# The last norm in two token tiles, and the experts' first query made one token tile at a time

## The chip, the cores and the metric

The kernel runs on one core of one Trainium2 chip. The metric is the device time of one execution in microseconds (us), the median of several. A profiled execution has a time of its own, and a span, which is the time from its first to its last recorded instruction. The engines are TensorE (PE: matmuls; PEld: its weight loads, which run beside the matmuls), VectorE (DVE), ScalarE (ACT), GpSimd (POOL) and SyncE (SP), which here issues every DMA.

## The reference, cut to what matters

256 tokens of 1024 features in float32 pass two attention layers, a third layer with windowed and neighbourhood attention, and then a layer of experts. The change lies between the third layer's output projection and the experts' first query:

```python
x = x + gate1[:, None, :] * (mixed @ w_out[layer])
h2 = modulate(rms_norm_2(x, norm2_g[layer]), shift2, scale2)
x = x + gate2[:, None, :] * peer(h2, w_query[layer], sub_keys[layer], u_experts[layer], v_experts[layer])
# in peer, per token: qh = xc @ w_query        (8 heads of 256)
#                     s1, s2 = qh halves against sub_keys, top 16 of each, top 16 of their sums
#                     z = xc @ u_sel ; a = gelu(z) * g ; out = a @ v_sel
```

The kernel does not gather experts: it computes z for all 128 x 128 experts (128 "u tiles") and multiplies by gains that are zero where an expert was not chosen.

## The kernel before, in words

The 256 tokens are two token tiles t = 0 and 1 of 128. The residual `x[t]` lies with tokens on partitions; the normed input `h` lies transposed, features on partitions, in 8 chunks k of 128 features, all 256 tokens along the free axis. A product in float32 accuracy is made of three matmuls (`mm3`, L239 to L241) of rounded halves: hi by hi, hi by lo, lo by hi. A weight from memory is loaded into one of 4 `raw` buffers (L229) and split: ScalarE casts hi (L186), VectorE subtracts lo = raw - hi (L211). There are 4 pairs of `hi`/`lo` buffers; further ones (`mo`) come from `more`.

The order of the work around the change:

- **The output projection** is `out_half(1)`. For t = 0, 1 and for c = 0, 1 (512 columns each) it makes 12 matmuls and then `finish(t, c, y)`: y times the row factor times the gate (L1280), x += y (L1283), and on ScalarE the square of x with its row sum (L262). Below, "the gate product" and "the add" of a (t, c) are L1280 and L1283.
- **The last norm** is `norm_T(5)`. For each t, `norm_diag` makes the reciprocal root of the sums in eight tiny VectorE operations (`rstd_x`, L271 to L278) and a diagonal matrix of it (L518). `norm_x` multiplies x with that matrix on TensorE, which scales and transposes (L525: 8 products for a token tile, two matmul records each, in two PSUM tiles of four feature chunks, called k4 = 0 and 1). `norm_h` applies scale and shift (k4 = 0 on ScalarE, L538; k4 = 1 on VectorE, L540) and splits the result into `hh` (L187 or L186) and `hl` (L211).
- **The experts' stage** `peer` first stores x in memory (L1351), loads constants and the keys (L1362, L1382), and makes `query(0)`: `projT` takes `wq[0]`, four split tiles of two feature chunks each, as the stationary operand and h as the moving one, 8 chunks x 2 halves m x 3 = 48 matmuls of 256 columns (all tokens). After it come u tile 0 (24 matmuls of 256 columns), the scores of query 0 (L1398), u tile 1, and so on without a break to the end of the kernel.

Tile's planner sets each engine's order of issue: among the operations that are ready in its model the one with the lowest priority number goes first, and the number grows in the order of the program. The layer's steps are listed in `ORDER['2']`; its last step, `O@5`, is `out_half(1)` with its numbers raised by 250, so that what comes after it in the program (the norm, the splits of `wq[0]`) goes ahead of it wherever it is ready. `add_manual_dep(..., NoSync, ...)` only puts one instruction behind another in the order of issue of the same engine; it adds no semaphore.

Of the kernel before, what the change touches and what calls it, by code (L numbers as in the profile page):

```python
# [15 lines left out]
OP = mybir.AluOpType  # L16
# [5 lines left out]
NK = 8  # L22
# [127 lines left out]
class Net:  # L150
    def __init__(self, ctx, tc, a):
        self.ctx, self.tc, self.nc, self.a = ctx, tc, tc.nc, a
        self.evn = 0
        self.spare = []
        self.oacc = {}
        self.paced = None
        self.lasts = []
        self.mods = {}
        self.ssx = None
# [36 lines left out]
    def split(self, raw, n=512, more=None):  # L196

        if more is None:
            hi = self.st.tile([128, 512], F32R, name="hi", tag="hi", bufs=self.nhl)
            lo = self.st.tile([128, 512], F32R, name="lo", tag="lo", bufs=self.nhl)  # L200
        else:
            hi, lo = more()
        i = self.split_to(hi[:, :n], lo[:, :n], raw[:, :n])
        self.lasts.append(i)
        if self.paced:
            self.paced(i)
        return hi, lo
# [306 lines left out]
    def norm_diag(self, t):  # L514

        self.rstd_x(self.rs[:, t:t + 1], self.ssx[:, 0, t:t + 1], self.ssx[:, 1, t:t + 1])
        dg = self.wp.tile([128, 128], F32, name="diag", tag="cpt", bufs=self.B("cpt"))
        self.nc.vector.tensor_scalar(dg, self.c("ident"), self.rs[:, t:t + 1], None, op0=OP.mult)  # L518
        return dg

    def norm_x(self, t, k4, dg):
# [20 lines left out]

    def norm_T(self, mod, ahead):

        self.norm_prep()
        for t in range(2):
            dg = self.norm_diag(t)
            pss = [self.norm_x(t, k4, dg) for k4 in range(2)]
            if t == 0:
                next(ahead)  # L550
            for k4 in range(2):
                self.norm_h(t, k4, pss[k4], mod, "av"[k4])
        self.ssx = None
        return self.h
# [42 lines left out]
    def proj(self, h, w, n=512):  # L597

        acc = [self.acc()[:, :n] for _ in range(2)]
        if isinstance(w, bass.AP):  # L600
            order = ((t, k, wt) for k, wt in enumerate(self.tiles(w, n)) for t in range(2))
        else:
            ws = next(w)
            order = ((t, k, wt) for t in range(2) for k, wt in enumerate(ws))
        for t, k, wt in order:
            self.mm3(acc[t], h, wt, (slice(None), k, slice(t * 128, t * 128 + 128)),
                     (slice(None), slice(0, n)), k == 0, k == NK - 1)
        return acc

    def projT(self, h, w, ps):  # L610

# [531 lines left out]
    def block2(self):  # L1143
        nc, v, a = self.nc, self.nc.vector, self.a
        with ExitStack() as es:
# [5 lines left out]
            h = self.norm_T(3, first)  # L1151
# [95 lines left out]
            def v_b():  # L1247
                o1 = self.proj(h, W[3])
                for t in range(2):
# [2 lines left out]
            self.steps("2", {"pA": ka_va, "qa": qa, "kb": kb, "qb": qb, "tb": tb, "vb": v_b, "sa": s_a, "sb": s_b,  # L1252
                             "oa": o_a, "ob": o_b})
            h = self.norm_T(5, iter([None]))
        for t in range(2):
            self.dump(f"x3_{t}", self.x[t])
        return self.gr, h

    def out_half(self, i):

        v = self.nc.vector
        oz, w, ssp = self.oz, self.wo, self.ssp
        if i == 0:
            self.gate = self.gate_rows(self.gr, self.ghalf)
        gate = self.gate
        rs = None
        if ssp is not None:
            rs = self.sm.tile([128, 2], F32, name="rab", tag="rab", bufs=2)
# [8 lines left out]
        def finish(t, c, y):  # L1277
            sl = slice(512 * c, 512 * c + 512)
            if rs is not None:
                v.scalar_tensor_tensor(y, y, rs[:, t:t + 1], gate[:, sl], op0=OP.mult, op1=OP.mult)  # L1280
            else:
                v.tensor_tensor(y, y, gate[:, sl], op=OP.mult)
            v.tensor_tensor(self.x[t][:, sl], y, self.x[t][:, sl], op=OP.add)  # L1283
            if i == 1:
                self.square(y, self.x[t][:, sl], self.ssx[:, c, t:t + 1])

# [2 lines left out]
        if i == 0:  # L1289
            for c in range(2):  # L1290
                acc = [self.acc() for _ in range(2)]
                for kw in weights(c):
                    for t in range(2):
                        product(t, [kw], acc[t])
                for t in range(2):
                    if merged:
                        self.oacc[t, c] = acc[t]
                    else:
                        finish(t, c, acc[t])
        else:  # L1300
            self.ssx = self.sm.tile([128, 2, 2], F32, name="ssx", tag="ssx", bufs=2)
            ws = [list(weights(0)), list(weights(1, self.more))]
            for t in range(2):
                for c in range(2):
                    acc = self.oacc[t, c] if merged else self.acc()
                    product(t, ws[c], acc)
                    finish(t, c, acc)

    def b2_out(self, t, ab, o, oz, ssp):
        nc, v = self.nc, self.nc.vector  # L1310
# [32 lines left out]
    def peer(self, r4, h):  # L1343
        nc, v, a = self.nc, self.nc.vector, self.a
# [16 lines left out]
        o, w = _CST["iota"]  # L1361
# [16 lines left out]
        with ExitStack() as er:  # L1378
# [9 lines left out]
            def query(hd):  # L1388

                acc = self.ps()  # L1390
                self.projT(h, a["wq"][hd], acc)
                qh = wp.tile([128, 2, 256], F32, name="qh", tag="qh", bufs=2)
                nc.scalar.copy(qh.rearrange("p a b -> p (a b)"), acc)
                uu(1)
# [288 lines left out]
```

## Time and profile before

| | |
|---|---|
| median of 3 runs | 1391.97 us (1389.85 to 1392.41) |
| the profiled execution: its time / its span | 1390.83 us / 1389.1 us |
| PE busy | 1339.5 us, 96% of the span, 8842 matmuls |
| PEld busy | 1126.9 us, 81% |
| DVE / ACT / POOL busy | 1023.2 us (74%) / 820.2 us (59%) / 21.8 us (2%) |
| granted TensorE clock, mean | 0.99 |
| DMA | 279.17 MB, mean 201 GB/s |

All times below are microseconds from the start of the span. A row of the timeline gives start, length, engine, line, operation, output tile <- input tiles, shapes and how many instructions were merged into the row; in square brackets stands how long the engine was idle before it, and what released it. A matmul's recorded length is its latency: matmuls are pipelined, and the distance from one start to the next says what one costs in a stream. PEclk is the TensorE clock that the throttle granted: 1.00 is 2.4 GHz, 0.50 is 1.2 GHz, and a value between says how much of the stretch lay at either level.

### The profile page before, as it was taken

What the parts mean: (1) busy time and instruction counts of PE and PEld (TensorE: products, weight loads), DVE (VectorE), ACT (ScalarE), POOL (GpSimd) and SP (SyncE); (2) the same over time, 40 slices, a digit from 0 to 9 for tenths busy, and PEclk for the clock granted to TensorE, in tenths of its full rate; (3) what the DMA queues carried; (4) which work ended last, traced back from release to release, by engine and by line L of the source; (5) the groups of instructions that cost most, each with busy time, mean ns of one, the idle gap of its engine ahead of it and who ended that gap; (6) DMA issues with size and microseconds to landing.
All of it is one profiled execution on the core that took longest, in us unless ns stands there. A gap on an engine that the chain in (4) does not pass through costs nothing.

```text
span 1389.1 us, 25082 instructions
## 1 busy us (share of the span) xinstructions
PE 1339.5 (96%) x8842; PEld 1126.9 (81%) x8842; DVE 1023.2 (74%) x2636; ACT 820.2 (59%) x1887; POOL 21.8 (2%) x27
## 2 busy tenths in 40 slices
PE   6998999999989997999999999999999999999997
PEld 2576775587667756999999999999998888888885
DVE  3595865688576657899999868888866666677777
ACT  3354666367457664555555668888865555555554
POOL 0000000000001100000000000000000000000001
PEclk9999999999999998999999999999999999999999
DMA  8688654742586774555555575455466656667773
GB/s 302 213 283 306 218 188 149 246 157 94 207 296 204 227 236 154 173 179 179 173 180 182 168 217 177 158 166 171 158 224 209 190 192 196 197 222 242 245 242 118
DMA packets 94876, 279.17 MB, mean 201 GB/s; under 512 B 11112, under 2 KB 30320, under 8 KB 94624
## 3 DMA queue, kind: packets, MB, share of 16 engines
q1 hardware_dynamic: 94752, 277.59, 60.6%
q8 instruction: 69, 1.13, 0.3%
q14 instruction: 55, 0.45, 0.1%
HBM read 267.80 MB, written 13.94 MB: 203 GB/s over the span
## 4 chain that ended last, share of the span: by engine, by line
PE 77%; DVE 3%; DMA 2%; ACT 1%; issue 0%; ACTq 0%; DVEq 0%
PE ps L241 18%; PE ps L240 18%; PE ps L239 18%; PE ps L1501 4%; PE acc L241 3%; PE acc L240 3%; PE acc L239 3%; DMA raw<-in_w1o 1%; PE psa L396 1%; PE ps L714 1%; PE ps L525 1%; DVE lo L211 1%; PE ps L709 1%; PE ps L1125 1%; PE ps L639 1%; PE ps L1398 1%
## 5 line engine op out<-in xcount | busy, mean ns | idle before, releaser
L186 ACT CAST hi<-raw 128x512 fp32r<-128x512 f32 (+1 forms) x700 | 429.4, 618 | 350.8 <-PE ps L240 147.8
L211 DVE TENSOR_TENSOR lo<-raw,hi 128x512 fp32r<-128x512 f32 (+1 forms) x700 | 479.8, 688 | 171.2 <-ACT hi L186 158.4
L239 PE MATMUL ps<-hh,hi 128*128 128x256 f32 x1160 | 333.6, 288 | 1.2 <-DVE hh L187 1.2
L240 PE MATMUL ps<-hl,hi 128*128 128x256 f32 x1160 | 329.0, 284 | 1.1 <-DVE hl L211 1.1
L241 PE MATMUL ps<-hh,lo 128*128 128x256 f32 x1160 | 329.0, 284 | 0.0
L239 PEld LDWEIGHTS ps<-hh,hi 128*128 128x128 f32 x1160 | 223.2, 192 | 1.4 <-DVE hh L187 1.4
L240 PEld LDWEIGHTS ps<-hl,hi 128*128 128x128 f32 x1160 | 223.1, 192 | 1.3 <-DVE hl L211 1.3
L241 PEld LDWEIGHTS ps<-hh,lo 128*128 128x128 f32 x1160 | 222.9, 192 | 0.0
L239 PE MATMUL ps<-hi,Ah 128*128 128x512 f32 x508 | 198.1, 390 | 0.0
L240 PE MATMUL ps<-lo,Ah 128*128 128x512 f32 x508 | 197.7, 389 | 0.0
L241 PE MATMUL ps<-hi,Al 128*128 128x512 f32 x508 | 197.6, 389 | 0.0
L240 PEld LDWEIGHTS ps<-lo,Ah 128*128 128x128 f32 x508 | 95.4, 188 | 20.2 <-DVE lo L211 0.2
L239 PEld LDWEIGHTS ps<-hi,Ah 128*128 128x128 f32 x508 | 95.4, 188 | 19.9 <-issue 0.2
L241 PEld LDWEIGHTS ps<-hi,Al 128*128 128x128 f32 x508 | 95.3, 188 | 19.8
L1500 ACT ACTIVATE og<-o,gT 128x128 f32<-128x128 bf16 x256 | 87.2, 394 | 4.1 <-DVE o L1498 0.3
L239 PE MATMUL acc<-hi,hh 128*128 128x512 f32 (+1 forms) x176 | 69.8, 402 | 4.3 <-DVE hh L187 3.1
L240 PE MATMUL acc<-lo,hh 128*128 128x512 f32 (+1 forms) x176 | 70.6, 402 | 2.4 <-DVE lo L211 2.4
L241 PE MATMUL acc<-hi,hl 128*128 128x512 f32 (+1 forms) x176 | 70.2, 400 | 0.0
L1501 PE MATMUL ps<-og,o 128*128 128x128 f32 x512 | 65.1, 275 | 0.0
L1501 PEld LDWEIGHTS ps<-og,o 128*128 128x128 f32 x512 | 61.4, 192 | 0.0
L396 PE MATMUL psa<-adaw,cond 128*32 128x256 f32 x640 | 48.5, 390 | 4.7 <-DMA adaw<-in_adaw 4.3
L1498 DVE TENSOR_TENSOR o<-iof,eT 128x512 bf16<-128x512 f32 x64 | 44.2, 691 | 8.2 <-ACT og L1500 7.5
(397 smaller groups left out, 1937.3 us busy)
## 6 DMA issues: line engine op xcount, KB each, us to landing
raw<-in_u SPq DMA_DIRECT2D x128, 512.0 KB, 3.5
raw<-in_v SPq DMA_DIRECT2D x128, 512.0 KB, 3.5
adaw<-in_adaw SPq DMA_DIRECT2D x86, 512.0 KB, 4.8
raw<-in_w SPq DMA_DIRECT2D x48, 512.0 KB, 3.6
raw<-in_wq SPq DMA_DIRECT2D x16, 512.0 KB, 3.5
zd<-ge SPq DMA_DIRECT2D x56, 128.0 KB, 1.7
ge<-zd SPq DMA_DIRECT2D x56, 128.0 KB, 3.4
raw<-in_adaw SPq DMA_DIRECT2D x10, 512.0 KB, 3.2
```

Of the source, the lines that this page charges most:

```text
L186: return self.nc.scalar.copy(out, in_)
L211: return self.nc.vector.tensor_tensor(lo, src, hi.bitcast(F32), op=OP.subtract)
L239: mm(out, a[0][asl], b[0][bsl], start=first, stop=False, **kw)
L240: mm(out, a[0][asl], b[1][bsl], start=False, stop=False, **kw)
L241: mm(out, a[1][asl], b[0][bsl], start=False, stop=last, **kw)
L396: i = nc.tensor.matmul(ps[32 * q:32 * q + 32, h * 256:h * 256 + 256], self.cond[:, ci + k, :], raw[:, q * 256:q * 256 + 256], start=(k == ...
L525: self.nc.tensor.matmul(ps[:, k * 128:k * 128 + 128], self.x[t][:, k4 * 512 + k * 128:k4 * 512 + k * 128 + 128], dg, start=(k == 0), stop= ...
L639: nc.tensor.transpose(pr[:P, i * 128:i * 128 + 128], s.rearrange("p a d -> p (a d)") if P == 128 else s, self.identr)
L709: nc.tensor.transpose(ps[:, r * 128:r * 128 + 128], P[a][r][:, br, kb, :], self.c("ident"))
L1498: v.tensor_tensor(o1, iob, eT[0][:, t0:t0 + 4, None].to_broadcast([128, 4, 128]), op=OP.is_equal)
L1500: nc.scalar.activation(og[:, j], o1[:, j], AF.Copy, scale=gT[:, t0 + j:t0 + j + 1])
L1501: nc.tensor.matmul(ps[:, j * 128:j * 128 + 128], o2[:, j], og[:, j], start=(j == 0), stop=(j == 3), skip_group_check=True)
```

## The change

`out_half(1)` of the third layer now makes, after the finishes of token tile 0, the norm's preparation and `norm_diag(0)`, so that this tile's diagonal (`dg0`) comes inside the output projection. The gate products of token tile 1 are put behind this diagonal in VectorE's order of issue. The first four splits after the norm (those of `wq[0]`) have their lo put behind the last add of token tile 0. `norm_T` uses the diagonal that is there and makes only the one of token tile 1. `query(0)` goes through `projT_first`: it splits all four tiles of `wq[0]` first, and then makes the product for the 128 tokens of t = 0 over all chunks, and after it for t = 1: 8 x 2 x 3 = 48 matmuls of 128 columns for each token tile, 96 in all.

```diff
@@ split
         i = self.split_to(hi[:, :n], lo[:, :n], raw[:, :n])
         self.lasts.append(i)
+        if self.behind:
+            self.tc.add_manual_dep(i.ins, self.behind.pop().ins.name, mybir.DependencyInfo(
+                mybir.DependencyClass.NoSync, mybir.DependencyReason.DATA), reason="order of issue")
@@ norm_diag
-        self.nc.vector.tensor_scalar(dg, self.c("ident"), self.rs[:, t:t + 1], None, op0=OP.mult)
+        self.diag0 = self.nc.vector.tensor_scalar(dg, self.c("ident"), self.rs[:, t:t + 1], None, op0=OP.mult)
@@ norm_T
-        self.norm_prep()
+        if self.dg0 is None:
+            self.norm_prep()
         for t in range(2):
-            dg = self.norm_diag(t)
+            dg = self.dg0 if t == 0 and self.dg0 is not None else self.norm_diag(t)
@@ new
+    def projT_first(self, h, w, ps):
+        ws = [wt for k4 in range(2) for _, wt in self.load_w(w[k4])]
+        for t in range(2):
+            for k in range(NK):
+                for m in range(2):
+                    o = 256 * m + 128 * t
+                    self.mm3(ps[:, o:o + 128], ws[k // 2], h, (slice(None), slice(k % 2 * 256 + m * 128, k % 2 * 256 + m * 128 + 128)),
+                             (slice(None), k, slice(t * 128, t * 128 + 128)), t == 0 and k == 0 and m == 0,
+                             t == 1 and k == NK - 1 and m == 1, skip_group_check=True)
@@ block2
             h = self.norm_T(5, iter([None]))
+            self.behind = [self.x0] * 4
@@ out_half, finish
-                v.scalar_tensor_tensor(y, y, rs[:, t:t + 1], gate[:, sl], op0=OP.mult, op1=OP.mult)
+                m = v.scalar_tensor_tensor(y, y, rs[:, t:t + 1], gate[:, sl], op0=OP.mult, op1=OP.mult)
+                if t and i == 1:
+                    self.tc.add_manual_dep(m.ins, self.diag0.ins.name, mybir.DependencyInfo(
+                        mybir.DependencyClass.NoSync, mybir.DependencyReason.DATA), reason="order of issue")
...
-            v.tensor_tensor(self.x[t][:, sl], y, self.x[t][:, sl], op=OP.add)
+            add = v.tensor_tensor(self.x[t][:, sl], y, self.x[t][:, sl], op=OP.add)
+            if t == 0:
+                self.x0 = add
@@ out_half, the loop over t
                     product(t, ws[c], acc)
                     finish(t, c, acc)
+                if t == 0 and self.L == 2:
+                    self.norm_prep()
+                    self.dg0 = self.norm_diag(0)
@@ peer, query
-                self.projT(h, a["wq"][hd], acc)
+                (self.projT if hd else self.projT_first)(h, a["wq"][hd], acc)
```

## Rows read from the trace of the kernel before

**Rows 1.** The page: span, and each engine's busy time.
```profile
span 1389.1 us, 25082 instructions
PE 1339.5 (96%) x8842; PEld 1126.9 (81%) x8842; DVE 1023.2 (74%) x2636; ACT 820.2 (59%) x1887; POOL 21.8 (2%) x27
```

**Rows 2.** Stretches: start:end length, busy time (instructions) per engine, clock, DMA share, GB/s.
```profile
560.00:1380.00 820.00, 820.00 (x5500) 758.67 (x5499) 650.39 (x1413) 511.51 (x1135) 3.00 (x3) 1.00 0.59 191
...
535.35:540.27 4.92, 0.00 (x0) 0.03 (x1) 4.77 (x18) 2.05 (x6) 0.00 (x0) 0.82 0.82 311
540.27:546.50 6.23, 6.22 (x32) 6.04 (x32) 3.29 (x11) 2.29 (x7) 0.00 (x0) 0.59 0.62 205
546.50:549.25 2.75, 0.39 (x2) 0.19 (x1) 2.41 (x6) 1.23 (x4) 0.00 (x0) 0.91 0.01 3
549.25:552.00 2.75, 2.75 (x13) 2.75 (x14) 1.28 (x3) 0.78 (x2) 0.00 (x0) 0.50 0.00 0
552.00:559.02 7.02, 7.02 (x59) 7.02 (x59) 3.35 (x5) 3.42 (x6) 0.00 (x0) 0.99 0.29 81
```

**Rows 3.** TensorE's timeline, 535 to 560.
```profile
540.27 6.23 PE L525 MATMUL ps<-diag,x 128*128 128x128 f32 x32 [4.94 <-DVE rx L274]
...
552.19 0.28 PE L241 MATMUL ps<-hh,lo 128*128 128x256 f32 x1
...
559.15 1.06 PE L1398 MATMUL ps<-keys,qh 128*128 128x128 f32 x8
```

**Rows 4.** Waits of PE from 535 to 565: waiter, releaser, total, times, longest.
```profile
PE ps L525 <- DVE rx L274: 4.9, 1, 4.9
PE ps L239 <- DVE hh L187: 1.2, 1, 1.2
PE ps L240 <- DVE hl L211: 1.1, 1, 1.1
```

**Rows 5.** VectorE's timeline, 530 to 552.
```profile
530.50 0.76 DVE L1280 SCALAR_TENSOR_TENSOR acc<-acc,rab,gate 128x512 f32<-128x512 f32 x1
531.17 2.80 DVE L211 TENSOR_TENSOR lo<-raw,hi 128x512 fp32r<-128x512 f32 x4
...
535.80 1.28 DVE L1283 TENSOR_TENSOR x<-acc,x 128x512 f32<-128x512 f32 x2
...
539.28 0.21 DVE L271 TENSOR_SCALAR rx<-ssx 128x1 f32<-128x1 f32 x1
...
539.84 0.29 DVE L518 TENSOR_SCALAR diag<-ident,rstd 128x128 f32<-128x128 f32 x1
...
541.13 0.29 DVE L518 TENSOR_SCALAR diag<-ident,rstd 128x128 f32<-128x128 f32 x1
...
544.56 0.68 DVE L211 TENSOR_TENSOR hl<-hf,hh 128x512 fp32r<-128x512 f32 x1
...
550.52 0.69 DVE L211 TENSOR_TENSOR hl<-hf,hh 128x512 fp32r<-128x512 f32 x1 [0.68 <-ACT hh L186]
```

**Rows 6.** ScalarE's timeline, 530 to 563.
```profile
530.50 2.73 ACT L186 CAST hi<-raw 128x512 fp32r<-128x512 f32 x4 [3.08 <-PE acc L241]
534.60 0.60 ACT L262 ACTIVATE acc<-x 128x512 f32<-128x512 f32 x1 [1.36 <-DVE x L1283]
...
551.83 0.62 ACT L186 CAST hi<-raw 128x512 fp32r<-128x512 f32 x1 [1.34 <-PE ps L240]
```

**Rows 7.** TensorE's timeline in the second layer: matmuls of 128 columns.
```profile
340.67 0.50 PE L733 MATMUL ps<-kT,qT 128*128 128x128 f32 x3
...
307.75 0.22 PE L733 MATMUL ps<-kT,qT 128*128 128x128 f32 x1
307.80 0.45 PE L240 MATMUL acc<-lo,hh 128*128 128x512 f32 x1
```

**Rows 8.** SyncE's DMA issues, 530 to 570.
```profile
536.51 2.32 SPq L1351 DMA_DIRECT2D xd<-x  x2
...
539.34 0.88 SPq L1382 DMA_DIRECT2D keys<-in_keys  x1
```

More of the change, by code (lines that the diff above doesn't have):

```diff
@@ L156, in __init__ @@
         self.paced = None
+        self.behind = []
+        self.dg0 = None
         self.lasts = []
```

## The prediction

> **What bounds the kernel now.** I read the page first: TensorE is busy for 96% of the span [rows 1], so nothing counts that does not shorten TensorE's own work or one of its few gaps. Next come the stretches: from 560 to 1380 TensorE is busy for 820.00 of 820.00 us at full clock [rows 2]. Whatever happens before 560 is therefore worth exactly the shift of the moment at which this unbroken stream begins. I put that moment, E, at the first matmul of u tile 0, which follows the 48 of query 0. From 552.19 on, the fifteenth of them [rows 3], matmuls start every 7.02 / 59 = 0.119 us [rows 2]; the forty-ninth is 34 later, so E = 552.19 + 34 x 0.119 = 556.2. The scores at 559.15, behind the 24 of u tile 0, confirm it: 559.15 - 24 x 0.119 = 556.3 [rows 3]. I use 556.2.
>
> The stretches and TensorE's waits then say what lies ahead of E. TensorE has nothing to do from 535.35 to 540.27, waits 4.9 us for the reciprocal root of the norm, makes the norm of both token tiles in 6.23 us, and waits once more for hh (1.2) and hl (1.1) [rows 2, 4]. VectorE is busy for 4.77 of the 4.92 us of the long wait [rows 2]: this gap is VectorE's work, not a latency. It has two parts there that the change can move: the four lo of the first query's weights, 2.80 us from 531.17, which push the first add back, and the finishes of token tile 1, which lie ahead of the chain of tile 0 [rows 5]. The clock is part of the price: it falls within the long wait (0.82), is 0.59 over the norm, and again 0.50 when the query goes on at 549.25 [rows 2].
>
> **The change part by part.**
>
> *The first diagonal earlier.* Before, the gate product of (0, 0) starts at 530.50 [rows 5]. Two gate products and two adds at 0.64 to 0.76 each [rows 5] end at about 533.3 when nothing is between them. The four lo are now behind that; their casts are ready at 530.50 + 2.73 = 533.2 [rows 6]. Their priority numbers are lower than those of the output projection, raised by 250, and so I expect the four ahead of the chain, as VectorE has nothing else while ScalarE squares: up to 2.8 us, to 536.1. The chain takes 541.13 - 539.28 = 1.85 us to the diagonal, and 540.27 - 539.84 = 0.43 us from the diagonal's start to TensorE [rows 3, 5]. TensorE starts the norm of tile 0 at 536.1 + 1.85 + 0.43 = 538.4; before, at 540.27. The other end: if the lo stay behind the chain, it starts one square (0.60 [rows 6], with its read-out about 0.8) after 533.3, and TensorE at 536.4. I take 538.3, near the late end, because of the numbers.
>
> *What is late next.* From TensorE's start to the end of hl for the first half (k4 = 0) of tile 0 took 544.56 + 0.68 - 540.27 = 4.97 us [rows 3, 5], at half clock. The eight records in that path cost about 0.2 us each there (6.23 / 32 = 0.195, [rows 3]) and would cost 0.119 at full clock, 0.6 less. TensorE's gap ahead of the norm shrinks from 4.9 to 3.0 us, so I leave both open: the first query can begin at 542.7 to 543.3, I take 542.9.
>
> *The query in two halves.* 48 matmuls of 256 columns at 0.119 were 5.7 us. Now there are 96 of 128 columns. The second layer has such matmuls in a row: three in 0.50 us, the last of which lasts 0.22 to 0.28, so one every 0.11 to 0.14 us at full clock [rows 7]; half the columns are no cheaper, since each record has a weight load of its own (8842 of either, [rows 1]). The bounds: 0.05 us between such a matmul and the next where a 512-column one had gone before [rows 7], and 2.75 / 13 = 0.212 if a stretch is at half clock [rows 2]. I take 0.115, from the row that is a plain stream: 96 x 0.115 = 11.0 us, 5.3 more than before.
>
> The TensorE page of the Trainium skill ("TensorE: Matmul & The Clock Gate", section "Back-to-back issue gap") gives about 81 ns for a sustained pair of weight load and 128-column matmul. By it the 96 would be 7.8 us and not 11.0; the row is of this kernel's own number format and stands against it.
>
> *The norm of tile 1.* It now comes after two gate products, two adds, a square and the chain, all behind the first diagonal, and among the 3 us of VectorE's share in the norm of tile 0. Before, its diagonal started 1.29 us after the first one (541.13 against 539.84 [rows 5]). Now four operations (2.7), a square with read-out (0.8) and the chain (1.85) make 5.4 us after the first one's start at 537.9: 543.3, or as late as 546 where norm operations go between. TensorE then needs 16 records, 1.9 us at full clock, and the last hl came 550.52 + 0.69 - 543.4 = 7.8 us after its start (540.27 + 6.23 / 2 = 543.4, [rows 3, 5]), about 7 at a higher clock: h is complete at 551 to 553, no earlier than before (551.2). The half for tile 0 is meant to fill TensorE up to then.
>
> *The clock.* The query went on at 549.25 after a gap with 0.39 us of work in 2.75, and 13 matmuls ran at 0.212 instead of 0.119, 1.2 us lost [rows 2]. After the norm of tile 0, TensorE has a gap of the same kind (from about 540.2 to 542.9); I charge the same 1.2 us.
>
> *The rest.* The second copy of x is stored when its add is done, some 3 us later than 537 to 538; behind it on SP's queue wait the constants and the keys (539.34 [rows 8]). The keys are first read at 559.15 [rows 3], so 13 us or more cover it; if they were late, every microsecond would count. All four hi/lo pairs are now held until the second half of the query, so that the first cast of u tile 0, at 551.83 before [rows 6], waits for 12 matmuls of that half: about 551.5 + 1.4 = 552.9. Cast and lo (0.62 + 0.69 [rows 5, 6]) make it 554.3, before E; uncovered it would be 1.3 us per split. The preparation of the norm only names buffers.
>
> *Sum.* TensorE has no gap left from 542.9 on if the order fits: 542.9 + 11.0 + 1.9 (norm of tile 1) + 1.2 (clock) = 557.0. By the other bound, h complete at 552 and the last 24 matmuls, 552 + 24 x 0.115 = 554.8: TensorE's own work ends last. E moves by 557.0 - 556.2 = +0.8 us. The profiled execution took 1390.83 us, 1.7 more than its span, and lies 1.1 below the median; on the median the forecast is 1391.97 + 0.8 = 1392.8, within 0.2% (2.8 us), about what a measurement of this kernel can tell from no change. The wait for the norm gets shorter, and the second set of weight loads eats what was won.
>
> **The rivals.**
>
> *Faster: the short halves hide wholly.* If the chain goes ahead of the lo (TensorE at 536.4) and the clock stays at 1.00, the query begins at 536.4 + 4.97 - 0.6 = 540.8 and E = 540.8 + 11.0 + 1.9 = 553.7: -2.5 us, 1389.5; with a late drop of the clock less. For it: TensorE then idles only 1.1 us before the norm instead of 4.9. Against: the priority numbers. Chance 0.15.
>
> *Faster: the weight load hides.* If, as next to 512-column matmuls [rows 7], a short matmul costs well under 0.115, TensorE's work stops being the bound and h does: with 0.05, E = 552 + 24 x 0.05 = 553.2, -3.0 us, 1389.0. Against: the plain stream [rows 7]. Chance 0.08. By the Trainium skill's page named above, with its 81 ns, it would be 552 + 1.9 = 553.9, and no row here shows that pace.
>
> *Slower: the norm of tile 1 at the wrong place in TensorE's fixed order.* Its 16 records are issued in an order laid down beforehand with modelled times. If the model holds short matmuls for cheap, or the second diagonal for late, the 48 of tile 0 go ahead: they end at 542.9 + 5.5 + 1.2 = 549.6, the norm starts then, the last hl is ready 7 us later at 556.6, and E = 556.6 + 24 x 0.115 = 559.4: +3.2 us, 1395.2. If it puts the norm ahead of all 48, TensorE waits for the diagonal: from 546 on 1.9 + 11.0 + 1.2 give E = 560.1, +3.9. It decides as soon as the norm's start is more than 2 us off the moment its diagonal comes. Chance 0.20.
>
> *The diagonal is not earlier.* If other VectorE work fills the place and TensorE starts at 540.27 as before: the query at 545.2, E = 545.2 + 11.0 + 1.9 + 1.2 = 559.3, +3.1 us, 1395.1. Against: the order behind the diagonal binds. Chance 0.05.
>
> **How the numbers follow.** Forecast 0.52, with its own range of 1.7 us to either side (pace 0.11 to 0.125 is -0.5 to +1.0, clock 0 to 2.4, start of the query 0.5). The first rival mostly ends inside 0.2%, a third of it beyond; the second likewise half. Together, with the faster tail of the forecast: faster 0.17. The two slow cases end just beyond 0.2% for the greater part: slower 0.21. Same 0.62. The range takes in the fast rivals at 1389 and the slow ones at 1396.
>
> **What would show it.** Right: TensorE's first norm matmul 2 to 4 us earlier, 96 short matmuls at about 0.11 us, their 16 norm records between them, and u tile 0 within 2 us of 556.2. Wrong: short matmuls at 0.05 to 0.08; norm records behind the 48th; clock 1.00 throughout; keys or u splits in TensorE's waits; any difference after E, which would come from another order in the stream and which I hold for nothing.

## The result, and the profile after

The changed kernel took 1400.55 us (median of 5 runs, 1397.11 to 1410.96); the kernel before, beside it, 1392.25 us. The ratio is 1.0065 with a 95% interval of 1.0041 to 1.0088. Three later series of the same kernel gave 1.0028 [1.0007, 1.0049], 1.0056 [1.0031, 1.0082] and 1.0079 [1.0046, 1.0112]: slower each time, with a wide scatter that turns out to be part of the answer. The forecast was 1392.8, no change; the measured time lies above the whole range.

The page of the profile after, to be read against [rows 1]: 48 more matmuls and weight loads, 5.8 us more busy time, 9.6 us more span.

```profile
span 1398.7 us, 25177 instructions
PE 1345.3 (96%) x8890; PEld 1133.9 (81%) x8890; DVE 1023.7 (73%) x2636; ACT 820.3 (59%) x1887; POOL 21.6 (2%) x27
```

TensorE's timeline of after, against [rows 3]. First the last matmul of the output projection, then the norm of each token tile, the first, the fourth and the last short matmul of the query, the first of u tile 0, the scores.

```profile
539.25 0.39 PE L247 MATMUL acc<-mo,ozl 128*128 128x512 f32 x1
541.87 3.62 PE L531 MATMUL ps<-diag,x 128*128 128x128 f32 x16 [2.23 <-DVE diag L524]
551.37 3.75 PE L531 MATMUL ps<-diag,x 128*128 128x128 f32 x16 [5.88 <-DVE diag L524]
554.77 0.45 PE L245 MATMUL ps<-hh,hi 128*128 128x128 f32 x1
...
555.45 0.28 PE L245 MATMUL ps<-hh,hi 128*128 128x128 f32 x1
...
565.73 0.28 PE L247 MATMUL ps<-hh,lo 128*128 128x128 f32 x1
565.85 0.33 PE L245 MATMUL ps<-hh,hi 128*128 128x256 f32 x1
...
568.76 1.06 PE L1426 MATMUL ps<-keys,qh 128*128 128x128 f32 x8
```

Where a profile's last output matmul starts differs from one execution to the next, in kernels whose order up to there is the same (534.95 and 535.48 in two profiles of before; 539.25, 537.57, 540.92 and 535.69 in four of the change). So I count every time from that start, written as +t. Before: norm at +5.32, scores at +24.20. After: norm of tile 0 at +2.62, of tile 1 at +12.12, query at +15.52, u tile 0 at +26.60, scores at +29.51. From the scores to the end it is 829.9 us in both (1389.1 - 559.15 and 1398.7 - 568.76). Of the 9.6 us between the two spans, 5.3 arise between the last output matmul and the scores, and 4.3 lie ahead of it.

TensorE's waits in that stretch make a single row, where [rows 4] had three; it sums up two waits (8.1 us), and the longer (5.9) is the one for the second diagonal:

```profile
PE ps L531 <- DVE diag L524: 8.1, 2, 5.9
```

Stretches of after, against [rows 2] (start:end, length, TensorE's busy time and records, clock, DMA share, GB/s). The norm of tile 0 runs at 0.54, that of tile 1 at 0.50; the query is at full clock from 557, and the stream behind it has no gap, as before.

```profile
541.80:545.50 3.70, 3.62 (x16) 0.54 0.37 130
545.50:551.30 5.80, 0.00 (x0) 0.77 0.44 121
551.30:554.70 3.40, 3.33 (x15) 0.50 0.69 282
554.70:557.00 2.30, 2.30 (x19) 0.84 0.00 0
557.00:565.80 8.80, 8.80 (x81) 1.00 0.02 4
...
569.00:1389.00 820.00, 820.00 (x5504) 1.00 0.61 191
```

VectorE's timeline of after, against [rows 5]. The four lo stand behind the adds of tile 0, then comes the first chain. The hl at 546.83 is the last operand that the query's first matmuls (tile 0, the first four chunks) need. The add of (1, 1), at 547.75, stands behind the norm operations of tile 0, and with it the second chain and the second diagonal.

```profile
537.32 2.49 DVE L217 TENSOR_TENSOR lo<-raw,hi 128x512 fp32r<-128x512 f32 x4
539.72 0.21 DVE L277 TENSOR_SCALAR rx<-ssx 128x1 f32<-128x1 f32 x1
...
541.43 0.29 DVE L524 TENSOR_SCALAR diag<-ident,rstd 128x128 f32<-128x128 f32 x1
541.64 1.41 DVE L1299 SCALAR_TENSOR_TENSOR acc<-acc,rab,gate 128x512 f32<-128x512 f32 x2
542.96 0.68 DVE L1306 TENSOR_TENSOR x<-acc,x 128x512 f32<-128x512 f32 x1
545.53 0.73 DVE L546 TENSOR_SCALAR hf<-ps,gs,cols 128x128 f32<-128x128 f32 x2 [1.89 <-PE ps L531]
...
546.83 0.68 DVE L217 TENSOR_TENSOR hl<-hf,hh 128x512 fp32r<-128x512 f32 x1
...
547.75 0.68 DVE L1306 TENSOR_TENSOR x<-acc,x 128x512 f32<-128x512 f32 x1
548.51 0.69 DVE L217 TENSOR_TENSOR hl<-hf,hh 128x512 fp32r<-128x512 f32 x1
549.22 0.21 DVE L277 TENSOR_SCALAR rx<-ssx 128x1 f32<-128x1 f32 x1
...
550.93 0.29 DVE L524 TENSOR_SCALAR diag<-ident,rstd 128x128 f32<-128x128 f32 x1
```

### The profile page after: what moved, and what is told of

It is laid out like the page before. It is cut to its first block, busy times and chain, and to the rows that moved or that the text cites. A ratio compares the mean times of both kernels' runs of the same rounds, so it can differ in the third digit from the quotient of the medians.

```text
span 1398.7 us, 25177 instructions
## 1 busy us (share of the span) xinstructions
PE 1345.3 (96%) x8890; PEld 1133.9 (81%) x8890; DVE 1023.7 (73%) x2636; ACT 820.3 (59%) x1887; POOL 21.6 (2%) x27
## 3 DMA queue, kind: packets, MB, share of 16 engines
q8 instruction: 70, 1.15, 0.3%
## 4 chain that ended last, share of the span: by engine, by line
PE 75%; DVE 3%; DMA 3%; ACT 1%; issue 0%; DVEq 0%; ACTq 0%
PE ps L247 18%; PE ps L246 18%; PE ps L245 18%; PE ps L1529 4%; PE acc L245 3%; PE acc L246 3%; PE acc L247 3%; DMA adaw<-in_adaw 2%; DMA raw<-in_w1o 1%; PE psa L402 1%; PE ps L531 1%; PE ps L732 1%; DVE lo L217 1%; PE ps L727 1%; PE ps L657 1%; PE ps L1426 1%
## 5 line engine op out<-in xcount | busy, mean ns | idle before, releaser
L245 PE MATMUL ps<-hh,hi 128*128 128x256 f32 (+1 forms) x1176 | 337.5, 287 | 0.0
L247 PE MATMUL ps<-hh,lo 128*128 128x256 f32 (+1 forms) x1176 | 332.8, 283 | 0.0
L246 PE MATMUL ps<-hl,hi 128*128 128x256 f32 (+1 forms) x1176 | 332.6, 283 | 0.0
```

The costliest lines, as they stand in the source:

```text
L245: mm(out, a[0][asl], b[0][bsl], start=first, stop=False, **kw)
L246: mm(out, a[0][asl], b[1][bsl], start=False, stop=False, **kw)
L247: mm(out, a[1][asl], b[0][bsl], start=False, stop=last, **kw)
```

## The experiments

My theory after this profile: (A) TensorE makes the norm of tile 1 ahead of all 96 short matmuls, so nothing fills the wait for it; (B) the short matmuls cost TensorE time of their own; (C) the waits bring TensorE to half clock. Rivals: the extra matmuls explain everything, without A; or the moved lo and the diagonal are to blame.

Overview. "Norm 0", "norm 1" and "query" are the starts in the profile from the last output matmul; "rest" is the span from there to the end, which leaves out the scatter ahead of it. Ratios are to the kernel before in the same session.

| kernel | norm 0 / norm 1 / query | rest | median (n) | ratio [95%] |
|---|---|---|---|---|
| before, first profile | 5.32 / - / 12.78 | 854.2 | 1392.25 (5) | |
| ctl_before | 5.33 / - / 12.29 | 853.2 | 1390.43 (10) | 0.9991 [0.9974, 1.0007] |
| the change | 2.62 / 12.12 / 15.52 | 859.5 | 1400.55 (5) | 1.0065 [1.0041, 1.0088] |
| ctl_after | 2.62 / 11.34 / 14.75 | 869.2 | 1395.53 (10) | 1.0028 [1.0007, 1.0049] |
| after_b | 2.62 / 11.55 / 14.96 | 869.2 | 1398.89 (12) | 1.0056 [1.0031, 1.0082] |
| after_c | 2.62 / 12.16 / 15.56 | 859.5 | 1399.96 (8) | 1.0079 [1.0046, 1.0112] |
| q256 | 2.61 / 11.59 / 15.75 | 856.8 | 1397.76 (10) | 1.0030 [1.0011, 1.0049] |
| q256_b | 2.63 / 11.89 / 16.06 | 856.8 | 1393.82 (12) | 1.0014 [0.9993, 1.0035] |
| q256_c | 2.62 / 10.52 / 14.69 | 855.7 | 1395.41 (12) | 1.0023 [1.0004, 1.0043] |
| half_only | 5.33 / - / 10.52 | 854.2 | 1394.1 (10) | 1.0016 [0.9997, 1.0034] |
| after_fin | 2.62 / 10.50 / 13.72 | 857.3 | 1399.41 (5) | 1.0076 [1.0050, 1.0102] |
| early_q | 2.61 / 10.52 / 5.80 | 859.7 | 1399.5 (7) | 1.0060 [1.0039, 1.0081] |
| early_fin | 2.62 / 10.19 / 5.81 | 860.3 | 1398.14 (10) | 1.0058 [1.0036, 1.0079] |
| after_warm | 2.62 / 10.45 / 12.25 | 855.8 | 1394.72 (10) | 1.0024 [1.0003, 1.0046] |
| warm | 5.33 / - / 12.53 | 851.2 | 1388.92 (12) | 0.9983 [0.9964, 1.0001] |
| lo_x0 | 4.74 / - / 12.21 | 853.6 | 1390.81 (12) | 1.0010 [0.9994, 1.0027] |
| lo_diag1 | 3.34 / - / 10.0 | 850.4 | 1388.3 (12) | 0.9978 [0.9961, 0.9995] |
| lo_warm | 3.35 / - / 10.55 | 849.1 | 1388.51 (12) | 0.9980 [0.9967, 0.9992] |

### The two kernels once more

> The kernel before, unchanged, as a control. Time 1391 to 1393. In the two profiles compared so far the changed kernel is 4.3 us late already at the last matmul of the output projection (539.25 against 534.95), where both programs issue the same instructions in the same order, and another 5.3 us late from there to the first matmul of u tile 0. Theory A (the second part alone is the change's work, the first is scatter between executions): this profile shows the stretch from the last output matmul to E at 21.3 again, within 0.5, and the time ahead of it anywhere between 534 and 540. Theory B (the change also slows what lies ahead of it): the time ahead stays within 1 us of 535.

> The changed kernel, unchanged, as a control. Time 1397 to 1402. Theory A: the last output matmul lies between 534 and 540, and 26.6 us (within 1) lie from it to E; the difference of the times to the kernel before then is about 5 to 6 us when the upstream scatter is averaged. Theory B: the last output matmul at 538 to 540 once more, difference 8 to 10 us.

The first takes the same time as before. Both expected stretches from the last output matmul to u tile 0 missed, and neither theory had foreseen the cause: in ctl_before it is 19.55 us instead of 21.3, as its query runs at full clock from 549.5 on; in ctl_after it is 35.27 instead of 26.6. The clock of ctl_after is 0.50 from the end of the norm of tile 0 until the first 256-column matmuls have run; the 96 short ones start 0.213 apart ((572.63 - 570.71) / 9), not 0.112 as in the first profile of the change ((565.73 - 555.45) / 92). TensorE's timeline and a stretch of ctl_after:

```profile
570.71 0.41 PE L247 MATMUL ps<-hh,lo 128*128 128x128 f32 x1
...
572.63 0.41 PE L247 MATMUL ps<-hh,lo 128*128 128x128 f32 x1
572.84 0.52 PE L245 MATMUL ps<-hh,hi 128*128 128x256 f32 x1
...
575.29 0.30 PE L247 MATMUL ps<-hh,lo 128*128 128x256 f32 x1
```
```profile
553.00:572.00 19.00, 19.00 (x91) 0.50 0.09 27
```

TensorE is busy without a break for these 19 us, and the clock does not come back in them.

### The query's form: half_only and q256

half_only is the kernel before with only the query in two halves; q256 is the change with only the query as before.

```
 half_only:  -  self.projT(h, a["wq"][hd], acc)
             +  (self.projT if hd else self.projT_first)(h, a["wq"][hd], acc)
 q256:       the same two lines the other way round, in the changed kernel
```

> The kernel before with nothing changed but query 0, made as 96 matmuls of 128 columns. In one profile of the change the clock rose to 1.00 at the start of its 96 short matmuls; in the control it stayed at 0.50 through all 96 (0.213 us each) and rose 2 us after the first matmuls of 256 columns. Theory E (short matmuls, each with its own weight load, cannot be relied on to bring the clock back, so the query costs 10.8 us at one level and up to 20.5 at the other): from the last output matmul to E it takes 25 to 28 us if the clock comes back early, 34 to 37 if not, against 19.5 and 21.3 of before; over the runs the mean is 4 to 10 us slower than before and the spread above 8 us. Rival F (only the place of the norm of tile 1 hurts, short matmuls are worth their price): 0 to 3 us slower, spread as before.

> The change with query 0 made for all 256 tokens at once again (48 matmuls of 256 columns); the norm of tile 1 stays behind. Theory A (in TensorE's order the norm of tile 1 stands ahead of all of the query, so that the halves hide nothing and only cost 96 weight loads): h is complete some 19 us after the last output matmul, the query follows, and E comes 23.0 to 24.5 us after that matmul instead of 26.6: 2 to 3.5 us faster than the change, still 2 to 3 us slower than before. Rival C (the halves do hide work behind the norm of tile 1): no faster than the change.

half_only ends where before does (rest 854.2 against 854.2 and 853.2), and its ratio, 1.0016 [0.9997, 1.0034], cannot be told from one. I had put 25 us or more from the last output matmul to u tile 0; it is 21.28: in this profile the clock is back at 1.00 before the short matmuls begin, and they do not bring it down. Rival F came true. The query begins 1.8 to 2.3 us earlier, because its first half needs only tile 0; the waits of [rows 4] for hh and hl are gone. TensorE's timeline and the stretches of half_only show the norm flowing into the query and the clock at 1.00 from there:

```profile
545.21 5.44 PE L525 MATMUL ps<-diag,x 128*128 128x128 f32 x32 [4.94 <-DVE rx L274]
550.40 0.31 PE L239 MATMUL ps<-hh,hi 128*128 128x128 f32 x1
```
```profile
545.88:548.88 3.00, 3.00 (x16) 0.51 1.05 340
548.88:551.88 3.00, 3.00 (x29) 1.00 0.07 25
551.88:554.88 3.00, 3.00 (x29) 1.00 0.00 0
```

So the extra matmuls alone do not explain the loss. q256 has no extra matmul and is still slower than before, 1.0030 (q256_b and q256_c below: 1.0014 and 1.0023, the first of them not clear of one): the split norm costs by itself. Its u tile 0 comes at +24.03, within what I expected. TensorE's timeline of q256 shows the same wait of 5.88 us, and behind it a query that begins at half clock:

```profile
550.87 3.75 PE L531 MATMUL ps<-diag,x 128*128 128x128 f32 x16 [5.88 <-DVE diag L524]
555.03 0.58 PE L245 MATMUL ps<-hh,hi 128*128 128x256 f32 x1 [0.41 <-DVE hh L189]
```

### The second diagonal: after_fin

The VectorE share of the norm of tile 0 is put behind the last add of tile 1.

```
+   if mod == 5 and t == 0:        # hf of k4 = 1 on VectorE
+       add_manual_dep(i.ins, self.x1.ins.name, NoSync)   # x1: the last add of out_half(1)
```

> The changed kernel, with the VectorE part of the norm of token tile 0 (hf, hh, hl) put behind the last add of token tile 1, so that the two products and two adds of tile 1 come in a row. Theory 'VectorE's fixed order holds the second diagonal up': the add of (1,1) comes 2 to 3 us earlier, TensorE's norm of tile 1 starts at +9.3 to +10 (11.3 and 12.1 in the two profiles of the change), and the stream begins 1.5 to 2.5 us earlier at the same clock: +24 at a clock that comes back, +34 at one that stays at half; ratio 1.000 to 1.003. Rival 'the second diagonal is not the bound': the query still waits for the last hl of tile 1, which comes no earlier because the norm operations of tile 0 are now behind; the stream within 0.5 us of the change's, ratio 1.003 to 1.0065.

VectorE's and TensorE's timelines of after_fin: the two adds of tile 1 now come in a row, the diagonal's start moves from +11.68 to +10.06, and the wait from 5.88 to 4.73.

```profile
542.16 1.28 DVE L1309 TENSOR_TENSOR x<-acc,x 128x512 f32<-128x512 f32 x2
...
548.51 0.29 DVE L524 TENSOR_SCALAR diag<-ident,rstd 128x128 f32<-128x128 f32 x1
```
```profile
548.95 3.47 PE L531 MATMUL ps<-diag,x 128*128 128x128 f32 x16 [4.73 <-DVE diag L524]
```

Norm 1 came 1.6 us earlier than in the first profile of the change, 0.5 later than I expected, and the rest shrank by 2.2 us (857.3). Not all of that is the order. The wait of 5.88 is the same in all four profiles of the change and all three of q256, and norm 1 starts there as much later as norm 0 takes longer: 2.02 us and +10.52 in q256_c (TensorE's timeline of q256_c below), 3.62 us and +12.12 in the change. Norm 0 takes 3.14 us in after_fin; of the 1.6 us, 1.15 are the shorter wait, the order's share, and the remaining 0.5 are the clock.

```profile
550.05 3.76 PE L531 MATMUL ps<-diag,x 128*128 128x128 f32 x16 [5.88 <-DVE diag L524]
```

The times do not follow: 1.0076, two of the five runs at 1404.8 and 1404.9. The shift is shown in the profile; a gain in time is not.

### The change as it was meant: early_q and early_fin

In the changed kernel the bank for the query's sum comes from a PSUM pool (`pp2`, L1381) that is opened only after the norm's pool has been closed (L1380). In early_q the sum lies in a bank of the earlier pool; early_fin is early_q and after_fin together.

```
+   acc = self.acc()                                 # ahead of peer, in the pool of the norm
+   self.projT_first(h, a["wq"][0], acc)
+   self.qh0 = self.raw()[:, 0:512]...               # its read-out, in a raw buffer
+   nc.scalar.copy(self.qh0, acc)
```

> The change, with query 0 accumulating in a bank of the PSUM pool that the third layer uses, ahead of that pool's close, instead of in the pool that is opened after it; its result goes through a raw buffer to the scores. Nothing else differs. In the planned order 17 matmuls of the first half now stand ahead of the norm of tile 1, none did before. Theory A (the close of the old pool, not h and not the diagonal, kept the query behind the norm): the 17 run in the gap of 5.9 us ahead of the norm of tile 1, E moves 2 to 4 us forward against the change. Rival D (the query waits for all of h by data): the 17 wait as well, the norm of tile 1 is held up behind them, E is no earlier.

> The changed kernel with two edits together: the VectorE part of the norm of token tile 0 behind the last add of token tile 1, and the first query's sum in a bank of the PSUM pool that is open before the norm, its read-out in another buffer, so that 16 or so of its short matmuls can stand ahead of the norm of tile 1. If the place of the norm of tile 1 were all that is wrong, this is the change as it was meant: the norm of tile 1 without a wait of more than 1 us, the query's last matmul at +20 to +22, ratio 0.998 to 1.001. Theory 'the clock and the second set of weight loads cost more than the order gives back': the norm's wait is gone, yet the 96 cost 11 us or more and the query's last matmul comes at +22 to +24; ratio 1.002 to 1.005.

Now 17 (early_q) and 16 (early_fin) short matmuls do stand ahead of the norm of tile 1, which none did in the change; TensorE's timeline of early_fin has the query's start, the norm of tile 1 with a wait of only 1.52, and u tile 0:

```profile
541.83 0.33 PE L245 MATMUL acc<-hh,hi 128*128 128x128 f32 x1 [1.16 <-DVE hh L189]
...
546.21 3.75 PE L531 MATMUL ps<-diag,x 128*128 128x128 f32 x16 [1.52 <-DVE diag L524]
...
560.72 0.39 PE L245 MATMUL ps<-hh,hi 128*128 128x256 f32 x1 [1.19 <-ACT hi L188]
```

The ratio is 1.0058, no better than the change. The wait is shorter by 4.4 us, but norm 1 runs at half clock (3.75 us for 16 records; 2.05 in after_warm below), 80 short matmuls still lie behind it, and the query's last comes at +23.2. u tile 0 starts at +24.70 (early_q: +25.08, 1.5 us earlier than in the change, not the 2 to 4 that I expected). The 1.19 us ahead of it are this edit's own cost: the casts of its weights stand behind the read-out of the query's sum. And that wait is followed by a second drop of the clock, where the change's first profile is at 1.00; a stretch of early_fin:

```profile
562.00:564.00 2.00, 2.00 (x12) 0.50 0.40 102
```

From the start of u tile 0 to the end early_fin takes 835.6 us, the change 832.9. An estimate without both costs: u tile 0 at +23.4 and 832.9 behind it make 856.2, that is some 3 us less than the change and still 2 to 3 more than the two profiles of before. So the wrong place of norm 1 is real and worth some 3 us, but mending it, with only a third of the first half ahead, does not make the change pay. No run has the mended order without the edit's own costs.

### The clock: fillers, and a count

Matmuls of 512 columns whose result is not read are put into the gaps: after_warm is the change with 8 ahead of norm 0 and 24 ahead of norm 1; warm is the kernel before with 18 ahead of the norm and 14 behind it.

```
+   w = self.pp.tile([128, 512], F32, name="psa", bufs=1)
+   for _ in range(n): nc.tensor.matmul(w, self.identr, <ozh, 512 columns>)   # behind the last matmul of that place
```

> The change with 32 matmuls of 512 columns added whose result nobody reads: 8 behind the output projection and 24 between the norms of the two token tiles, where TensorE stands idle for 2.2 and 5.9 us. Theory E: TensorE stays at 1.00 through the norm of tile 1 and the query; from the last output matmul to E 24 to 25.5 us in every profile, the time 2 to 6 us below the change and the spread that of before; still 3 to 4 us above before, as 96 short matmuls stand behind the norm of tile 1. Rival G (the clock follows the short matmuls themselves): the clock falls again within the query, no gain.

> The kernel before with 32 matmuls of 512 columns added whose result nobody reads: 18 behind the output projection, 14 behind the norm. Theory E: the clock stays at 1.00 from the output projection to E; the norm takes 3.8 instead of 6.2 us and the first 13 matmuls of the query 0.119 instead of 0.212 us: E 2 to 3 us earlier than in the first profile of before, 18 to 19 us after the last output matmul. Rival G (the extra matmuls only occupy TensorE when it is wanted): E the same or 1 us later.

after_warm: the norms take 2.02 and 2.05 us and the waits are 0.37 and 0.21 (TensorE's timeline below); the clock is 1.00 throughout. The rest is 855.8, 3.6 less than in the change: that is what half clock cost in the change's first profile, where the norms' 3.62 and 3.75 alone are 3.3 more. In warm the clock is 1.00 from the norm on and u tile 0 comes at +18.38, as expected; its ratio, 0.9983 [0.9964, 1.0001], cannot be told from one.

```profile
540.29 2.02 PE L538 MATMUL ps<-diag,x 128*128 128x128 f32 x16 [0.37 <-DVE diag L524]
542.07 5.84 PE L530 MATMUL psa<-ozh,identr 128*128 128x512 f32 x24
548.12 2.05 PE L538 MATMUL ps<-diag,x 128*128 128x128 f32 x16 [0.21 <-DVE diag L524]
```

What was still open is whether the short form or the wait keeps the clock down for a whole query. Four more runs counted it:

> The changed kernel again, for its runs' mean granted clock. Theory 'the short matmuls keep the half clock': some 2 in 10 runs have a mean clock of 0.983 or less and take over 1404 us, the others stay under 1402; median ratio 1.002 to 1.004.

> The changed kernel a third time, as the run above: some 2 in 10 runs at a mean clock of 0.983 or less and over 1404 us.

> The changed kernel with the first query in 48 matmuls of 256 columns, again. Theory 'the short matmuls keep the half clock': no run over 1402 us and none below 0.983. Rival 'the gap ahead of the second token tile's norm does it': the same share of runs over 1404 us as in the change itself, some 2 in 10.

> The changed kernel with the first query in 48 matmuls of 256 columns a third time: by the theory no run over 1402 us, by the rival some 2 in 10 over 1404 us.

Of the 35 runs of the change, 9 took over 1404 us, with a mean granted clock of 0.976 to 0.984 over the execution; of 34 runs of q256 none took over 1401.3 (lowest clock 0.982), of 124 runs of before in these sessions none over 1398.7, of 10 each of half_only and after_warm none over 1400.1. By 9 in 35 one would expect 8 to 9 in the 34, and 5 in the 20. As far as these counts go, it takes both, a wait of TensorE ahead of the query and its short form. It need not be the long wait of 5.88: early_fin, with 1.16 ahead of the query and 1.52 ahead of norm 1, has 3 such runs in 10 and after_fin, with 4.73, has 2 in 5 (1404.8 to 1405.9 us, clock 0.981 to 0.983), early_q none in 7; none of these five long runs was profiled. (The medians of after_b and after_c lie above what I expected, and one run of q256_c, 1400.4 us at 0.982, is below the clock that I expected, though not long.) after_b's profile is such a run; its stretch of 20 us at half clock is the whole query:

```profile
557.00:577.00 20.00, 20.00 (x95) 0.50 0.09 26
```

The means give the parts: before 1391.8 (124 runs), q256 1395.2 (34), the change 1400.2 (35), of which the 26 shorter runs 1397.1 and the 9 longer 1408.9. The split norm costs 3.5 us, the short form 1.9, and the long half clock another 3.0 on average (11.8 in a quarter of the runs). 96 x (0.213 - 0.112) = 9.7 is most of the 11.8. The 1.9 is the weakest of the three: against q256 beside them, the shorter runs were 2.2 us faster in the session of ctl_after and 3.2 us slower in that of after_b and after_c.

### The lo: lo_x0, lo_diag1, lo_warm

All three are the kernel before. lo_x0 takes the one edit that puts the four lo behind the last add of tile 0; lo_diag1 puts them behind the second diagonal; lo_warm is lo_diag1 with 8 and 14 fillers.

```
 lo_x0:    +  self.behind = [self.x0] * 4        # as in the change
 lo_diag1: +  self.behind = [self.diagi] * 4     # diagi: the diagonal of t = 1
```

> The kernel before, with only the part of the change that puts the four lo behind the last add of token tile 0. Theory 'VectorE's work ahead of the first diagonal sets the gap': the four lo still lie ahead of the chain, only two operations later, so the norm starts at +5.0 to +5.6 and the stream at +19.5 to +21.5, as before; ratio 0.999 to 1.001. Rival 'the place does it': the squares of token tile 0 come earlier, the norm starts at +3.3 to +4 as with the lo behind the second diagonal, and the ratio is 0.998.

> The kernel before with one edit of the change turned: the four lo of the first query's weights are put behind the second diagonal in VectorE's order (the change puts them behind the last add of tile 0), where VectorE waits 2.5 us for ScalarE. Query and norm as before. Theory A (VectorE's 2.8 us of lo ahead of the norm are on the path): the norm starts 2.3 to 2.8 us earlier after the last output matmul (2.5 to 3.0 instead of 5.3), E 1.5 to 3 us earlier; 1389 to 1390.5 against before in the same session, at the edge of what can be told. Rival H (the lo are late for the query instead): TensorE waits for lo, no gain.

> The kernel before, with the four lo of the first query's weights put behind the second diagonal, and with 8 and 14 further 512-column matmuls on TensorE ahead of the norm and between its two tiles; the result of these 22 is not read. Theory 'VectorE's gap and the clock are two separate costs': the norm of tile 0 starts 3.3 us after the start of the last output matmul, as with the lo alone, the clock over norm and query is above 0.8, the first query begins at +8.5 to +9.5 and the stream after it at +15.5 to +16.5 (17.2 with the lo alone, 18.3 with the fillers alone); ratio 0.995 to 0.998. Rival 'one cost': the fillers only take the place of waiting and delay the norm; the stream at +17 or later, ratio 0.998 or above.

lo_x0 cannot be told from before (1.0010 [0.9994, 1.0027]), and the rival that blames the moved lo falls, as far as the move alone goes: the norm starts at +4.74, a little before what I expected; the lo are behind two adds, but still ahead of both diagonals. lo_diag1 takes them out of VectorE's way: TensorE's and VectorE's timelines of lo_diag1 show a wait of 2.95 instead of 4.94, and a first lo at 542.19, while TensorE is on the norm. The norm starts at +3.34, later than the +2.5 to +3.0 that I expected; u tile 0 comes at +17.25, where the two profiles of before have +21.31 and +19.55. One wait, of 0.3 us, names a lo: rival H costs that and no more.

```profile
540.76 5.44 PE L531 MATMUL ps<-diag,x 128*128 128x128 f32 x32 [2.95 <-DVE rx L276]
547.42 0.38 PE L243 MATMUL ps<-hh,hi 128*128 128x256 f32 x1 [1.22 <-DVE hh L188]
548.34 0.39 PE L244 MATMUL ps<-hl,hi 128*128 128x256 f32 x1 [0.54 <-DVE hl L215]
```
```profile
541.99 0.29 DVE L522 TENSOR_SCALAR diag<-ident,rstd 128x128 f32<-128x128 f32 x1
542.19 0.68 DVE L215 TENSOR_TENSOR lo<-raw,hi 128x512 fp32r<-128x512 f32 x1
```

It has the lowest median of all, 1388.3 us, 0.9978 [0.9961, 0.9995], and beats both kernels. lo_warm keeps the clock at 1.00 and has the smallest rest, 849.1, but its time is the same as lo_diag1's (0.9980): with the fillers the first query starts at +10.55 instead of +10.0. I had expected +8.5 to +9.5; the stream came at +16.4, as expected.

## Why the prediction was wrong

- **The first diagonal earlier: right.** TensorE was to start the norm 1.97 us earlier, at +3.35; it started at +2.62. The lo did go ahead of the chain; the wait ahead of the norm is 2.23, forecast 3.0.
- **The failed step: "TensorE has no gap left from 542.9 on if the order fits", and with it "The half for tile 0 is meant to fill TensorE up to then".** No short matmul stands ahead of the norm of tile 1. The forecast let the query begin at 542.9, +7.95, and its operands were there nearly then: the hl of tile 0 ends at 547.51, +8.26. But the query begins at +15.52, behind a wait of 5.88 and the norm of tile 1. Of the 4.55 us by which u tile 0 is later than forecast (+26.60 against +22.05), 4.2 arise here: TensorE was to be busy from +7.95 on and is so from +12.12 on. That none came ahead did not depend on modelled times, as my rival had it, but on the bank: with the sum in the earlier pool, 17 and 16 came ahead (early_q, early_fin). That they were no more than that, although TensorE then waited 1.80 and 1.52 us with more of the first half to do, is left to the planner's order. That the pool's closing is what puts the query behind the norm is read from the code and fits these two runs; it acts through the order of issue, since at run time the query does not wait for the old pool's last reads (it starts at 554.77, and VectorE reads the norm's PSUM tile at 556.31). I had read `query` without asking when its PSUM tile can exist.
- **The rival that came true** is the second half of "the norm of tile 1 at the wrong place", given 0.20 for both halves: norm ahead of all 48, E = 560.1, that is +25.15. Measured +26.60. Its terms: the norm begins at +12.12, not by +11.05 at the latest, since the add of (1, 1) stands behind norm work on VectorE (1.15 us by after_fin) and norm 0 ran at half clock (3.62 us instead of 2.02); and it takes 3.40 to the query's start, not 1.9, at half clock. By it the time would have been 1391.97 + 3.9 = 1395.9. The 35 runs of the change lie 4.3 us above that in the mean, and 3.0 of these are the long half clock of nine of them. That this rival's number was not far off is partly luck: its norm was too early and too short by 2.6 us, and the 1.2 us that it charged for the clock within the query were 0.1 in the first profile.
- **The norm of tile 1: late by 0.6 to 3.3 us.** I gave its diagonal 543.3 to 546, +8.35 to +11.05; it came at +11.68.
- **The query's pace: right at full clock.** 0.112 against the forecast 0.115, and 0.213 at half clock. The Trainium skill ("TensorE: Matmul & The Clock Gate", section "Back-to-back issue gap") has about 81 ns for such a pair; the trace does not agree, and no run here has a query of short matmuls at that pace.
- **The clock: mis-sized.** I charged 1.2 us once. In the first profile it cost 3.6 (after_warm), since both norms run at half clock too; in a quarter of the runs, by the two that were profiled, it stayed at half through the query for 10 us more. My own range for it, "clock 0 to 2.4", was set from a row in which 256-column matmuls follow [rows 2], and none of my rows of before has a query of short ones behind a gap.
- **Keys and splits: right.** The keys are issued at 549.31 and read at 568.76 (SyncE's timeline of after below); no wait of TensorE names them or the split of u tile 0. After E nothing changed.

```profile
549.31 0.77 SPq L1410 DMA_DIRECT2D keys<-in_keys  x1
```

What stays open is why the clock returns in about three quarters of the runs and not in the others. The four profiles of the change differ already in the gap ahead of norm 1: where the clock comes back early in the query, it had been at 1.00 for some 3 us of that gap (545.5 to 548.5 in the first profile, likewise in after_c); in ctl_after and after_b it is 0.50 throughout the gap. Two profiles of each kind show no cause. The 4.3 us ahead of the last output matmul I take for scatter: over all 18 profiles that matmul starts between 533.87 and 540.96, and of the kernels before with nothing but later edits half_only has it at 539.88 and warm at 540.96. The two profiles of before alone (534.95 and 535.48) would not show that.

## What to carry to other kernels

A stage that is to fill a wait must be able to begin in it: ask for each of its operands and for its output bank when it exists, before adding up engine time. Splitting a product to start half of it earlier pays its weight loads twice and turns TensorE's one wait for the diagonals into two; here, moving four VectorE operations out of the path of the wait, with nothing split, gave some 3 us (0.7 to 5.4 by the interval) that the split could not. When a change is in a stretch where TensorE's clock moves, one profile is a sample: count the runs and their mean clock.

## What the runs showed of the hardware

At half clock matmuls of 128 and of 256 columns both start every 0.213 us (ctl_after); at full clock every 0.112 and 0.119. Half the columns save 6% at most here. A stream of 96 such short matmuls, TensorE busy for 20.00 of 20.00 us, did not bring the clock back in two of the four profiles of the change, and in both it rose 2.0 to 2.5 us after the first 256-column ones began (572.84 to 575.3 in ctl_after). It is not that short matmuls never do so: in the other two profiles, and in early_q and early_fin, the clock rose among them (after three at half clock in the first profile, at 555.45, and after some eight in early_fin). The same stream behind a norm without a gap was at 1.00 from its first matmul (half_only, one profile).
